# The last tile of the last projection in two token halves, in a two-layer trunk kernel

## The chip, the core and the metric

The kernel runs on one core of one Trainium2 chip. Its engines are TensorE (matmuls, with a separate queue of weight loads), VectorE, ScalarE, GpSimd and SyncE (which issues the DMAs here); the profile calls them PE, PEld, DVE, ACT, POOL and SP. The metric is the device time of one execution in microseconds; lower is better.

## What is computed

Two layers of a trunk over 256 latent tokens with a prefix of 256 context tokens, 1024 channels, in float32. Each layer mixes tokens (a convolution branch and neighbourhood attention, gated) and then channels (a gated MLP with a convolution of width 3 ahead of the activation). The change touches only what ends the last layer: the MLP's down projection, the gated residual and the final RMSNorm of the latent tokens.

```python
def conv_ffn(h, w_up, dw, dw_b, w_down):
    u = dwconv1d(h @ w_up, dw, dw_b)
    a, g = jnp.split(u, 2, axis=-1)
    return (jax.nn.silu(g) * a) @ w_down          # w_down: 2816 x 1024
...
        x = x + g2 * conv_ffn(h2, w_up[l], ffn_dw[l], ffn_dw_b[l], w_down[l])
...
    return rmsnorm(x, final_norm_g)               # x / sqrt(mean(x^2) + 1e-6) * g, over channels
```

## The kernel before

Everything is kept with channels on partitions and tokens along the free axis: the stream `x` is eight tiles `x[n]` of 128 channels by 512 columns, the 256 latent tokens (`LAT`) and then the 256 context tokens (`CTX`). In the last layer the context is no longer needed after its keys and values, so the column range `CTX` of `x` is free there.

Products go through `mm3` (lines 178 to 181): float32 operands are split into a high part, rounded to the type `F32R`, and a low rest, and each product is three matmuls, high by high, high weights by low data, low weights by high data. The weights arrive in units of 128x1024 (eight blocks of 128x128). `wunit` issues the unit's DMA on SP's queue into `raw` (four buffers), ScalarE casts it to `whi` (line 160) and VectorE subtracts to make `wlo` (line 161); both have four buffers.

The down projection of the last layer has eight output tiles `n`, each a sum over `KF` = 22 blocks `k` of the hidden activations `fh[k]`, `fl[k]` (128 hidden channels by 256 tokens, high and low part). In the last layer the whole projection is one pass over `n` in the loop that begins with `for streams, ns in`, with 256 columns a matmul. Block `t = n * KF + k` of the weights is in unit `t // 8`. After every fourth `k` a `slot()` lets side work take a step, here the dot products (line 271) for the gate vector of this sub-layer. After the last `k` of a tile, `residual` (line 898) makes x = x + gate * product on VectorE and hands the result to `SumSq.add`, which accumulates squares: ScalarE squares, VectorE adds to the accumulator `acc`. With `apart` set, the last tile's squares are made by VectorE (line 314) and kept as a part of their own in `parts`, so that the sums over partitions can start with the accumulator. Then line 1078 scales the tile by the final gain on ScalarE, into the free columns `CTX` of `x[n]`. Behind tile 6 one small instruction loads ScalarE's table for the square root.

Behind the loop comes the final norm, for all 256 tokens at once. Line 1094 sums the squares over the partitions: a matmul with the squares of 128 tokens as weights and a column of ones as data, for two parts and two token halves. Line 1098 takes the root on ScalarE, line 1099 the reciprocal on VectorE. Now there is one factor per token, with tokens on partitions; the transposes of line 1102 spread it over all partitions into the bank `po`. Line 1107 multiplies the eight scaled tiles by it, 256 tokens at a time, and SP issues the output: two DMAs of 128 KB (line 1109) and three of 256 KB (line 1111).

Each engine runs its instructions in the order in which they are written, and waits at an instruction until what that needs is there; loads of weights may run ahead of the matmuls before them.

Of the kernel before, what the change touches and what calls it, by code (L numbers as in the profile page):

```python
# [8 lines left out]
F32 = mybir.dt.float32  # L9
F32R = mybir.dt.float32r  # L10
BF16 = mybir.dt.bfloat16
AF = mybir.ActivationFunctionType
ALU = mybir.AluOpType
AX = mybir.AxisListType

P = 128
D = 1024
KD = D // P
DEPTH = 2
S = 256  # L20
# [8 lines left out]
KF = FFN // P  # L29
# [3 lines left out]
LAT, CTX = slice(0, S), slice(S, 2 * S)  # L33

BADA, N1G, DW, DWB, LNG, LNB, N2G, FDW, FDB, NPAR = 0, 48, 56, 180, 184, 188, 192, 200, 332, 376


U_GLU0, U_V, U_IN, U_NA, U_CO, U_WO, U_UP, U_DN = 0, 2, 6, 36, 40, 44, 52, 96
# [7 lines left out]
def trunk(ctx: ExitStack, tc: tile.TileContext, xt, cvec, crow, wall, wada, params, bias_t, rope_t, out):  # L46
    nc = tc.nc
    pe, act, dve, pool, sp = nc.tensor, nc.scalar, nc.vector, nc.gpsimd, nc.sync
# [11 lines left out]
    def nm(s):  # L60
        uid[0] += 1
        return f"{s}_{uid[0]}"
# [3 lines left out]
    def psum(tag="main"):  # L66
        return psp.tile([P, 512], F32, tag=tag, bufs=BANKS[tag], name=nm(tag))

    def tmp(w=512):
        return tp.tile([P, w], F32, tag="t", bufs=5, name=nm("t"))  # L70

    def small(shape, tag, bufs=2):
        return tp.tile(shape, F32, tag=tag, bufs=bufs, name=nm(tag))

    def sl(w, i):
        return w[:, i * P : (i + 1) * P]
# [14 lines left out]
    def whole(g):  # L91

        while True:
            try:
                next(g)
            except StopIteration as e:
                return e.value

    def finish(g):
        for _ in g:  # L100
            pass
        if g in side:
            side.remove(g)


    start = ExitStack()
# [3 lines left out]
    par = cp.tile([P, DEPTH * NPAR + KD], F32, name="par")  # L110
    act.dma_start(par[:, :DW], params[:, :DW])
    ident = cp.tile([P, P], F32, name="ident")
    make_identity(nc, ident)
    one = cp.tile([P, 1], F32, name="one")
# [4 lines left out]
    eps = cp.tile([P, 1], F32, name="eps")  # L119
# [30 lines left out]
    def wparts(l, u, at=None, cuts=2):  # L150

        r = wp.tile([P, UW], F32, tag="raw", bufs=4, name=nm("raw"))
        hi = (at or wp).tile([P, UW], F32R, tag="whi", bufs=4, name=nm("whi"))
        lo = (at or wp).tile([P, UW], F32R, tag="wlo", bufs=4, name=nm("wlo"))
        cs = [slice(i * UW // cuts, (i + 1) * UW // cuts) for i in range(cuts)]
        for c in cs:
            lastdma[0] = sp.dma_start(r[:, c], wall[l, u][:, c])

        def split(c):
            act.copy(hi[:, c], r[:, c])  # L160
            dve.tensor_tensor(lo[:, c], r[:, c], hi[:, c].bitcast(F32), ALU.subtract)  # L161

        def more():
            for c in cs[1:]:
                split(c)

        split(cs[0])
        return (hi, lo), more

    def wunit(l, u, at=None, cuts=1):  # L170
        w, more = wparts(l, u, at, cuts)
        more()
        return w

    def cols(w, i):
        return sl(w[0], i), sl(w[1], i)

    def mm3(ps, w, xh, xl, start, stop):
        pe.matmul(ps, w[0], xh, start=start, stop=False)  # L179
        pe.matmul(ps, w[0], xl, start=False, stop=False)  # L180
        pe.matmul(ps, w[1], xh, start=False, stop=stop)  # L181

    def group(ps, ws, xh, xl, c):

        n = len(ws)
        for k in range(n):
            mm3(ps[:, c], ws[k], xh[k][:, c], xl[k][:, c], k == 0, k == n - 1)
            if k == n // 2 - 1 and c.stop - c.start > S:
                slot()
        slot()  # L190
        return ps

    def unit8(l, u, at=None):
        w = wunit(l, u, at)
        return [cols(w, i) for i in range(KD)]
# [85 lines left out]
    def mod2(l, part, k):  # L281
        return mods[l][:, part * KD + k, :]

    def mod(l, part, k, s):
        return mod2(l, part, k)[:, s : s + 1]
# [12 lines left out]
    x = [xp.tile([P, 2 * S], F32, name=f"x{k}") for k in range(KD)]  # L298
# [26 lines left out]
    def sum_squares(n, T, apart=False):  # L325

        at = tp.tile([P, 512], F32, tag="ss", name=nm("ss"))
        return [SumSq(T, at[:, i * T : (i + 1) * T], apart) for i in range(n)]
# [25 lines left out]
    def h_tiles():  # L354
        return [[hp.tile([P, 2 * S + 2], F32R, tag=f"h{i}{k}", name=nm("h")) for k in range(KD)] for i in range(2)]
# [176 lines left out]
    for k in range(KD):  # L532
        sp.dma_start(x[k], xt[k])
        q = tmp()
# [23 lines left out]
    for l in range(DEPTH):  # L558
        last = l == DEPTH - 1
        NS = 1 if last else 2  # L560
# [3 lines left out]
        with ExitStack() if last else start as e1a:  # L564
# [68 lines left out]
            with ExitStack() as e1b:  # L633
# [15 lines left out]
                if l == 0:  # L649
# [27 lines left out]
                    def more():  # L677
                        act.copy(wg[0][:, cuts[0]], rg[:, cuts[0]])
                        act.copy(pb, ps)
                        act.copy(wv[0][:, cuts[1]], rv[:, cuts[1]])  # L680
                        act.copy(wg[0][:, cuts[1]], rg[:, cuts[1]])
                        for w, r, c in ((wv, rv, cuts[0]), (wg, rg, cuts[0]), (wv, rv, cuts[1])):
                            low_part(w, r, c)
# [3 lines left out]
                    with tc.issue_after(queue[-1].ins):  # L687
                        ps = whole(sums)
                        queue.append(busy(5))
                    pb = tp.tile([P, 512], F32, tag="ss", name="rstd0")  # L690
# [41 lines left out]
                else:  # L732
                    sp.dma_start(rope, rope_t)
                    pg0 = [psum("sc") for _ in range(2)]
                    for uu in range(2):
                        wg = wunit(l, U_GLU0 + uu)
                        for i in range(2):
                            for kk in range(4):
                                k = 4 * uu + kk
# [59 lines left out]
                n = 0  # L799
# [16 lines left out]
            with ExitStack() as e1c:  # L816
# [71 lines left out]
                for n, pc in branch(U_CO, sh_, sl_):  # L888
                    t = tmp()[:, :T]
# [29 lines left out]
                sss = sum_squares(NS, S)  # L919
# [5 lines left out]
                for n in range(NB):  # L925
                    ps = group(psum(), unit8(l, U_WO + n), *z, ALL)
# [8 lines left out]
                for s in range(NS if held else 0):  # L935
                    for n, w in zip(range(NB, KD), held):
                        c = slice(s * S, (s + 1) * S)
                        ps = psum()
# [11 lines left out]
        with ExitStack() as e2:  # L950
            ef = e2.enter_context(tc.tile_pool(name=f"ef{l}", bufs=1))
# [20 lines left out]
            fh, fl = {}, {}  # L972
# [23 lines left out]
            if last:  # L996
# [3 lines left out]
                for k in range(KD):  # L1000
# [4 lines left out]
                    if k == 4:  # L1005
                        pb = whole(sums)
# [45 lines left out]
                    ffn_out(i - 3, pss[2 * i - 6], pss[2 * i - 5])  # L1052
            if not last:
                h1 = h_tiles()
            sss = sum_squares(NS, S, last)
            NB = 0 if last else KD - 2
            if not last:
                pace[0] = 0.55
# [4 lines left out]
            for streams, ns in [((0, 1), range(NB)), *(((s,), range(NB, KD)) for s in range(NS))]:  # L1063
                wu = None
                c = slice(streams[0] * S, (streams[-1] + 1) * S)
                for n in ns:
                    ps = psum()
                    for k in range(KF):
                        t = n * KF + k
                        if t % 8 == 0 or not wu:  # L1070
                            wu = wunit(l, U_DN + t // 8)
                        mm3(ps[:, c], cols(wu, t % 8), fh[k][:, c], fl[k][:, c], k == 0, k == KF - 1)
                        if k % 4 == 3:
                            slot()
                    for s in streams:
                        residual(sss[s], ps, 5, n, s, s * S)
                    if last:
                        scaled = act.mul(x[n][:, CTX], x[n][:, LAT], par[:, DEPTH * NPAR + n : DEPTH * NPAR + n + 1])
                        if n == KD - 2:
                            with tc.issue_after(scaled.ins):  # L1080
                                act.activation(small([P, 1], "wb", 4), one, AF.Sqrt)
                if not last and streams == (0,):
                    finish(ad)
                if not last and len(streams) == 1:
                    nl = norm(1, sss[streams[0]], 1, 0, N1G, h1, streams, streams[0])
                    add_side(nl)


            if last:
                std, rs = small([P, 2], "red"), small([P, 2], "rs")  # L1090
                pt = psum("pt")
                for i, p in enumerate(sss[0].parts):
                    for t in range(2):
                        pe.matmul(
                            pt[:, t : t + 1], sl(p, t), one, start=i == 0 and t == 0, stop=i == len(sss[0].parts) - 1,
                            skip_group_check=True,
                        )
                act.activation(std, pt[:, 0:2], AF.Sqrt, bias=eps, scale=1.0 / D)
                dve.reciprocal(rs, std)
                pb = psum("po")  # L1100
                for t in range(2):
                    pe.transpose(sl(pb, t), rs[:, t : t + 1].to_broadcast([P, P]), ident)
                for k in range(0, KD, 2):
                    y = tmp()
                    for i in range(2):
                        c = slice(i * S, (i + 1) * S)
                        dve.tensor_tensor(y[:, c], x[k + i][:, CTX], pb[:, LAT], ALU.mult)
                        if k == 0:
                            sp.dma_start(out[0][:, c], y[:, c])
                    if k:  # L1110
                        sp.dma_start(out[k // 2], y)


def _tiles(w):
# [110 lines left out]
```

## Time and profile before

| | us |
|---|---|
| median of 3 runs | 1131.16 |
| lowest, highest | 1129.35, 1134.31 |
| the profiled execution's own time | 1129.86 |
| its span, first to last instruction | 1128.1 |
| TensorE busy | 1113.2 |
| VectorE busy | 909.4 |
| ScalarE busy | 563.3 |
| mean granted TensorE clock | 0.997 of full speed |

In the profile's rows, "L181 PE MATMUL main<-fh,wlo 128*128 128x256 f32" is a matmul from line 181 into the tile `main`, with the weights `wlo` of 128 by 128 and data `fh` of 128 partitions by 256 columns. A number in square brackets, or the last column of a group, is how long the engine sat idle before, and who released it. In groups, the numbers behind the first bar are busy time in us and the mean duration of one in ns. In rows in order of time the first number is the start from the beginning of the span, the second the duration, both in us. Matmuls are pipelined: each lasts longer than the distance to the next, and a row's end is modelled. Plain f32 matmuls appear as two instructions each.

### The profile page before, as it was taken

Reading aid. Unit: us, or ns where it says so; the run is one execution under the profiler, and the core shown is the slowest. Engines: PE = TensorE matmul, PEld = TensorE weight load, DVE = VectorE, ACT = ScalarE, POOL = GpSimd, SP = SyncE. Lnnn points to the kernel's source line nnn. Section 1 sums busy time; section 2 is a strip of 40 time slices with the busy share of each in tenths; the row PEclk is TensorE's granted clock in tenths of the full one; section 3 lists DMA queues with packets and bytes.
Section 4 is the critical chain, followed back from the end, with each engine's and each line's share of the span. In section 5 each row is a group of like instructions: output and inputs, shape, how many; then the busy total and the mean of one; then the engine's idle time right before and its main releaser. Section 6 shows DMA issues by size and latency. Waiting matters only on the chain.

```text
span 1128.1 us, 17731 instructions
## 1 busy us (share of the span) xinstructions
PE 1113.2 (99%) x6828; PEld 963.1 (85%) x6828; DVE 909.4 (81%) x1631; ACT 563.3 (50%) x934; POOL 17.2 (2%) x24
## 2 busy tenths in 40 slices
PE   9999999999999999999999999999999999999997
PEld 6778777787789988888888888989898999999997
DVE  5689999685778788888898555789996898988773
ACT  4347657542333543434443223444677567766642
POOL 0000000000000000000000000000000000000000
PEclk9999999999999999999999999999999999999998
DMA  9823231636734344554556655545433575565771
GB/s 361 283 94 104 75 117 38 205 97 217 245 114 144 114 154 149 168 172 146 172 171 218 224 185 189 175 174 175 153 121 115 181 240 172 187 194 180 217 269 57
DMA packets 53941, 190.83 MB, mean 169 GB/s; under 512 B 6240, under 2 KB 6496, under 8 KB 53856
## 3 DMA queue, kind: packets, MB, share of 16 engines
q1 hardware_dynamic: 53568, 189.65, 51.6%
q8 instruction: 54, 0.88, 0.3%
q14 instruction: 31, 0.25, 0.1%
q10 hardware_dynamic: 288, 0.04, 0.0%
HBM read 188.62 MB, written 1.05 MB: 168 GB/s over the span
## 4 chain that ended last, share of the span: by engine, by line
PE 84%; DVE 10%; DMA 3%; ACT 2%; issue 1%; SPq 0%; DVEq 0%; ACTq 0%
PE main L179 25%; PE main L181 24%; PE main L180 24%; DVE cb L591 4%; PE main L644 4%; DVE wlo L161 2%; DMA raw<-in_wall 1%; PE sc L179 1%; PE sc L181 1%; PE sc L180 1%; PE po L202 1%; PE po L512 1%; DMA x<-in_xt 1%; DMA sb<-in_crow 0%; PE sc L440 0%
## 5 line engine op out<-in xcount | busy, mean ns | idle before, releaser
L179 PE MATMUL main<-h,whi 128*128 128x256 f32 (+1 forms) x1328 | 447.5, 338 | 0.0
L181 PE MATMUL main<-h,wlo 128*128 128x256 f32 (+1 forms) x1328 | 444.0, 335 | 0.5 <-DVE wlo L161 0.5
L180 PE MATMUL main<-h,whi 128*128 128x256 f32 (+1 forms) x1328 | 443.0, 334 | 0.0
L160 ACT CAST whi<-raw 128x1024 fp32r<-128x1024 f32 (+1 forms) x244 | 252.4, 1039 | 286.0 <-PE main L180 127.3
L161 DVE TENSOR_TENSOR wlo<-raw,whi 128x1024 fp32r<-128x1024 f32 (+1 forms) x244 | 293.5, 1209 | 113.9 <-ACT whi L160 107.3
L179 PEld LDWEIGHTS main<-h,whi 128*128 128x128 f32 x1328 | 249.8, 188 | 31.8 <-issue 3.9
L181 PEld LDWEIGHTS main<-h,wlo 128*128 128x128 f32 x1328 | 250.0, 189 | 28.7 <-DVE wlo L161 0.7
L180 PEld LDWEIGHTS main<-h,whi 128*128 128x128 f32 x1328 | 250.3, 189 | 27.9 <-issue 0.2
L591 DVE SCALAR_TENSOR_TENSOR cb<-u,par,cb 128x512 f32<-128x512 f32 (+1 forms) x240 | 140.4, 617 | 1.2
L271 DVE CUSTOM_DVE_ANT_0 t<-raw,sb,par 128x1024 bf16<-128x1024 f32 x100 | 126.8, 1279 | 1.0 <-ACT sb L255 0.8
L180 PE MATMUL main<-fl,whi 128*128 128x256 f32 (+1 forms) x386 | 123.1, 319 | 0.0
L179 PE MATMUL main<-fh,whi 128*128 128x256 f32 (+1 forms) x386 | 123.1, 319 | 0.0
L181 PE MATMUL main<-fh,wlo 128*128 128x256 f32 (+1 forms) x386 | 123.1, 319 | 0.0
L180 PEld LDWEIGHTS main<-fl,whi 128*128 128x128 f32 x386 | 72.8, 189 | 5.6
L181 PEld LDWEIGHTS main<-fh,wlo 128*128 128x128 f32 x386 | 72.8, 189 | 5.5
L179 PEld LDWEIGHTS main<-fh,whi 128*128 128x128 f32 x386 | 72.8, 189 | 5.5
L963 ACT ACTIVATE t<-main,par 128x512 f32<-128x512 f32 (+1 forms) x82 | 50.6, 668 | 40.0 <-PE main L181 39.8
L964 DVE SCALAR_TENSOR_TENSOR t<-main,par,t 128x510 f32<-128x510 f32 (+1 forms) x82 | 47.6, 616 | 10.5 <-ACT t L963 10.1
L967 DVE SCALAR_TENSOR_TENSOR t<-main,par,t 128x510 f32<-128x510 f32 (+1 forms) x82 | 46.6, 611 | 0.0
L366 ACT ACTIVATE h<-t,mod 128x256 fp32r<-128x256 f32 x56 | 25.2, 501 | 35.8 <-DVE t L365 35.8
L898 DVE SCALAR_TENSOR_TENSOR x<-main,mod,x 128x256 f32<-128x256 f32 x48 | 22.1, 480 | 23.4 <-PE main L181 23.2
L644 PE MATMUL main<-whi,h 128*128 128x512 f32 x128 | 40.5, 402 | 0.1
(221 smaller groups left out, 1193.1 us busy)
## 6 DMA issues: line engine op xcount, KB each, us to landing
raw<-in_wall SPq DMA_DIRECT2D x239, 512.0 KB, 4.2
raw<-in_wada SPq DMA_DIRECT2D x88, 512.0 KB, 4.4
bias<-in_bias_t SPq DMA_DIRECT2D x8, 640.0 KB, 4.3
row<-in_wada SPq DMA_DIRECT2D x8, 512.0 KB, 5.1
sb<-in_crow SPq DMA_DIRECT2D x5, 512.0 KB, 5.7
x<-in_xt SPq DMA_DIRECT2D x8, 256.0 KB, 4.1
raw<-in_wall SPq DMA_DIRECT2D x8, 256.0 KB, 7.3
out<-t SPq DMA_DIRECT2D x3, 256.0 KB, 2.1
```

Of the source, the lines that this page charges most:

```text
L160: act.copy(hi[:, c], r[:, c])
L161: dve.tensor_tensor(lo[:, c], r[:, c], hi[:, c].bitcast(F32), ALU.subtract)
L179: pe.matmul(ps, w[0], xh, start=start, stop=False)
L180: pe.matmul(ps, w[0], xl, start=False, stop=False)
L181: pe.matmul(ps, w[1], xh, start=False, stop=stop)
L271: dve.tensor_tensor_reduce(tmp().bitcast(BF16), r, v, 1.0, pr(l, BADA + n, 1), ALU.mult, ALU.add, mods[l][:, n, s : s + 1])
L366: high = act.activation(hi[:, c], y[:, c], AF.Identity, bias=b)
L591: dve.scalar_tensor_tensor(cb[j], src, w, cb[j], ALU.mult, ALU.add)
L644: mm = pe.matmul(pv[t], h1[n == 1][k][:, c], w[n == 2][:, b], start=k + n == 0, stop=k == KD - 1 and n == 2)
L963: act.activation(c, pv_, AF.Identity, bias=pr(l, FDB + t, 1), scale=w[1])
L964: dve.scalar_tensor_tensor(c[:, :, 1:], pv_[:, :, : S - 1], w[0], c[:, :, 1:], ALU.mult, ALU.add)
L967: dve.scalar_tensor_tensor(c[:, :, : S - 1], pv_[:, :, 1:], w[2], c[:, :, : S - 1], ALU.mult, ALU.add)
```

## The change

The loop over output tiles stops ahead of the last one (`n = 7`). That tile runs as two halves of 128 tokens: `half(0)` makes its 22 times 3 products for tokens 0 to 127, then update, scaling and squares of that half; `half(1)` does the same for tokens 128 to 255, with the same weight units, and between its products, behind `k = 7` and `k = 13`, come the norm factor and the output of the first half (`factor(0)`, `give(0)`). Behind the second half come `factor(1)` and `give(1)`. There are no slots within this tile.

The scaled tiles go to a new tile `xs`, laid out by token half, channel tile and token. With it one instruction multiplies four channel tiles of one half (512 elements) by the factor, which is read four times through a broadcast. The output has a layout of its own, in four pieces of 256 KB, two for each half, and the host's last rearrangement follows it. The sums of squares of tiles 0 to 6 use the accumulator alone. The scratch space for descriptors of dynamic DMAs is set to 1024.

```diff
-            sss = sum_squares(NS, S, last)
+            sss = sum_squares(NS, S)
+            if last:
+                xs = ef.tile([P, 2, KD, P], F32, name="xs")
...
                 for n in ns:
+                    if last and n == KD - 1:
+                        break
...
                     if last:
-                        scaled = act.mul(x[n][:, CTX], x[n][:, LAT], par[:, DEPTH * NPAR + n : DEPTH * NPAR + n + 1])
+                        g = par[:, DEPTH * NPAR + n : DEPTH * NPAR + n + 1]
+                        scaled = act.mul(xs[:, :, n, :], x[n][:, LAT].rearrange("p (h t) -> p h t", h=2), g)
...
             if last:
-                std, rs = small([P, 2], "red"), small([P, 2], "rs")
-                pt = psum("pt")
-                for i, p in enumerate(sss[0].parts):
-                    for t in range(2):
-                        pe.matmul(
-                            pt[:, t : t + 1], sl(p, t), one, start=i == 0 and t == 0, stop=i == len(sss[0].parts) - 1,
-                            skip_group_check=True,
-                        )
-                act.activation(std, pt[:, 0:2], AF.Sqrt, bias=eps, scale=1.0 / D)
-                dve.reciprocal(rs, std)
-                pb = psum("po")
-                for t in range(2):
-                    pe.transpose(sl(pb, t), rs[:, t : t + 1].to_broadcast([P, P]), ident)
-                for k in range(0, KD, 2):
-                    y = tmp()
...
+                n = KD - 1
+                g = par[:, DEPTH * NPAR + n : DEPTH * NPAR + n + 1]
+                units = {n * KF // 8: wu}
+                squares = []
+
+                def half(h, between=()):
+                    c = sl(x[n], h)
+                    ps = psum()[:, :P]
+                    for k in range(KF):
+                        t = n * KF + k
+                        if t // 8 not in units:
+                            units[t // 8] = wunit(l, U_DN + t // 8)
+                        mm3(ps, cols(units[t // 8], t % 8), sl(fh[k], h), sl(fl[k], h), k == 0, k == KF - 1)
+                        if k in between:
+                            between[k]()
+                    dve.scalar_tensor_tensor(c, ps, mod(l, 5, n, 0), c, ALU.mult, ALU.add)
+                    act.mul(xs[:, h, n, :], c, g)
+                    q = ef.tile([P, P], F32, name=f"sq{h}")
+                    dve.tensor_tensor(q, c, c, ALU.mult)
+                    squares.append(q)
+
+                rsh = []
+
+                def factor(h):
+                    std, rs = small([P, 1], "red"), small([P, 1], "rs")
+                    pt = psum("pt")
+                    for i, p in enumerate((sl(sss[0].acc, h), squares[h])):
+                        pe.matmul(pt[:, 0:1], p, one, start=i == 0, stop=i == 1)
+                    act.activation(std, pt[:, 0:1], AF.Sqrt, bias=eps, scale=1.0 / D)
+                    dve.reciprocal(rs, std)
+                    rsh.append(rs)
+
+                def give(h):
+                    pb = sl(psum("po"), 0)
+                    pe.transpose(pb, rsh[h].to_broadcast([P, P]), ident)
                     for i in range(2):
...
+                        y = tmp().rearrange("p (k t) -> p k t", k=4)
+                        dve.tensor_tensor(y, xs[:, h, 4 * i : 4 * i + 4, :], pb.unsqueeze(1).to_broadcast([P, 4, P]), ALU.mult)
+                        sp.dma_start(out[h, i], y)
+
+                half(0)
+                half(1, {7: lambda: factor(0), 13: lambda: give(0)})
+                factor(1)
+                give(1)
...
-    nc = bacc.Bacc("TRN2", target_bir_lowering=False, num_devices=1)
+    nc = bacc.Bacc("TRN2", target_bir_lowering=False, num_devices=1, dynamic_dma_scratch_size=1024)
...
-    out = nc.dram_tensor("out_0", (KD // 2, P, 2 * S), F32, kind="ExternalOutput").ap()
+    out = nc.dram_tensor("out_0", (2, 2, P, 4, P), F32, kind="ExternalOutput").ap()
```

More of the change, by code (lines that the diff above doesn't have):

```diff
@@ L1099, in trunk @@
-                dve.reciprocal(rs, std)
-                pb = psum("po")
-                for t in range(2):
-                    pe.transpose(sl(pb, t), rs[:, t : t + 1].to_broadcast([P, P]), ident)
-                for k in range(0, KD, 2):
-                    y = tmp()
-                    for i in range(2):
[L1106 to L1111, printed above, removed]
+                n = KD - 1
@@ L1223 @@
     got = r.results[0]["out_0"]
-    return np.ascontiguousarray(got.reshape(KD // 2, P, 2, S).transpose(0, 2, 1, 3).reshape(D, S).T).reshape(1, S, D).astype(f32, copy=False)
+    return np.ascontiguousarray(got.reshape(2, 2, P, 4, P).transpose(1, 3, 2, 0, 4).reshape(D, S).T).reshape(1, S, D).astype(f32, copy=False)
```

## The prediction

> **What bounds the kernel now.** I read the page first (busy time by engine, shares of the chain that ended last), then the chain of waits of the last 11 us, then the order of time on each engine there, and last the groups by shape for durations.
>
> ```profile
> PE 1113.2 (99%) x6828; PEld 963.1 (85%) x6828; DVE 909.4 (81%) x1631; ACT 563.3 (50%) x934; POOL 17.2 (2%) x24
> ...
> PE 84%; DVE 10%; DMA 3%; ACT 2%; issue 1%; SPq 0%; DVEq 0%; ACTq 0%
> ```
>
> TensorE is busy 99% of the span and carries 84% of the chain, so any step added to its stream goes into the time at its full length. The end is another matter:
>
> ```profile
> 1118.99 0.13 PE main L181
> ...
> 1119.15 0.49 DVE x L898
> ...
> 1119.67 0.44 DVE t L314
> ...
> 1120.15 0.62 PE pt L1094 x4
> ...
> 1120.85 0.27 ACT red L1098
> ...
> 1121.14 0.18 DVE rs L1099
> ...
> 1121.36 0.45 PE po L1102 x2
> ...
> 1121.83 0.42 DVE t L1107
> 1122.26 0.33 DVEq L1220
> 1122.59 1.99 DVE t L1107 x6
> ```
>
> After the last product ends at 1119.12 a strictly serial tail follows: update, square, sums over partitions, root, reciprocal, transposes, eight output products of VectorE up to 1124.58, then the transfers. The span ends at 1128.1, so the tail is 9.0 us: 5.46 to the last output product, 3.5 of transfer and closing behind it. That is all the change can attack; what it pays with is TensorE steps. The last tile's own products:
>
> ```profile
> 1111.12 0.28 PE L179 MATMUL main<-fh,whi 128*128 128x256 f32 x1
> 1118.83 0.28 PE L181 MATMUL main<-fh,wlo 128*128 128x256 f32 x1
> ```
>
> 22 k times 3 is 66 products; from the first start to the last are 65 steps in 7.71 us, 0.1186 us a product of 256 columns, or 7.83 for the tile. The durations in these rows (0.28) overlap; the step is what counts.
>
> **The change, part by part.**
>
> *1. 66 products of 256 columns become 132 of 128 (the main cost).* Each needs its own load of 128x128 weights, for half 1 loads them again. No product of float32r in the trace has fewer than 256 columns, so the step at 128 must be bounded. From below, the column rate:
>
> ```profile
> 301.12 0.39 PE L181 MATMUL main<-sh,wlo 128*128 128x512 f32 x1
> ...
> 302.95 0.39 PE L180 MATMUL main<-sl,whi 128*128 128x512 f32 x1
> ```
>
> Eight steps in 1.83 us are 0.229 for 512 columns, so 256 columns more cost 0.110 (0.43 ns each) and 128 columns would step at 0.1186 - 0.055 = 0.064. But the loads do not shrink:
>
> ```profile
> L202 PEld LDWEIGHTS po<-raw,sil 128*32 128x32 f32 x128 | 3.2, 109 | 4.0 <-issue 2.2 <-ACT whi L680 0.4
> L512 PEld LDWEIGHTS po<-pT,V 128*64 128x64 f32 x144 | 9.5, 136 | 5.4 <-issue 1.3
> L181 PEld LDWEIGHTS main<-fh,wlo 128*128 128x128 f32 x386 | 72.8, 189 | 5.5
> L1094 PEld LDWEIGHTS pt<-one,ss 128*128 128x128 f32 x4 | 0.5, 190 | 0.0
> ...
> 1118.83 0.53 PEld L1094 LDWEIGHTS pt<-one,ss 128*128 128x128 f32 x4
> 1120.14 0.52 PEld L1094 LDWEIGHTS pt<-one,t 128*128 128x128 f32 x4 [0.78 <-DVE t L314]
> ```
>
> A load lasts 109 ns for 32 columns, 136 for 64, 189 for 128: 80 ns for 96 columns more, 0.83 ns a column, so 128 columns occupy the loading path for 107 ns. The last two rows show the same thing as a step: with one moving column there is nothing to compute, yet four loads take 0.53 and 0.52, (0.53 - 0.19) / 3 = 0.113 and (0.52 - 0.19) / 3 = 0.110. Those loads are of plain f32, but last as long (190) as those of float32r (189). At 256 columns load and product cover each other; at 128 the product is the shorter, and the load sets the step. I take 0.112, from the row that it is nearest to: a stream of 128-column loads with too little product to cover them. Ends: 0.064 below; above, two passes as plain f32 has them at just this width:
>
> ```profile
> 6.46 1.06 PE L527 MATMUL pt<-one,t 128*128 128x128 f32 x8
> L527 PE MATMUL pt<-one,t 128*128 128x128 f32 x32 | 4.4, 280 | 0.7 <-DVE t L539 0.5 <-DVE t L542 0.2
> ```
>
> Eight instructions here are four products (two passes each): (1.06 - 0.27) / 7 = 0.113 an instruction, 0.225 a product. With 0.112: 132 x 0.112 = 14.78 against 7.83, **+6.95**. With 0.064: 8.45, +0.6. With 0.225: 29.7, +21.9.
>
> The Trainium skill, "TensorE: Matmul & The Clock Gate", section "LDWEIGHTS (loading the stationary operand)", puts a load at its columns divided by 1.2 GHz, whatever the rows, and so speaks against the change; the slope of 0.83 ns a column agrees with it, and by its figure alone (an estimate, 107 ns) the two halves would take 14.1 instead of 14.78.
>
> *2. The first half's norm on TensorE, inside the second half's products.* Four f32 instructions for the sums and one transpose now stand in the stream.
>
> ```profile
> 736.77 0.58 PE L336 MATMUL pt<-one,ss 128*128 128x1 f32 x4 [1.92 <-DVE ss L322]
> 737.41 0.28 PE L180 MATMUL sc<-h,whi 128*128 128x256 f32 x1
> ...
> 937.86 0.28 PE L181 MATMUL main<-h,wlo 128*128 128x258 f32 x1
> 937.98 0.38 PE L351 MATMUL po<-ident,rs 128*128 128x128 f32 x2
> ...
> 938.32 0.28 PE L180 MATMUL sc<-h,whi 128*128 128x258 f32 x1
> ```
>
> From the start of four such sums to the second product behind them is 0.64; less one product (0.119) they cost 0.52. Two transposes stretch two steps from 0.24 to 0.46, so 0.11 each. **+0.63.** Neither should wait: half 0's update and square end 0.7 us after its last product, the sums come 24 products (2.7 us) after it; root and reciprocal end about 0.5 after the sums, the transpose comes 18 products (2.0 us) after them. If that cover were gone, the products queued behind would wait in order. Ends: 0.4 (nothing but bare steps of 0.08) and 0.9 (0.05 for each of several waits).
>
> *3. The first half's output.* After the transpose 24 products (2.7 us) are left; two output products of VectorE take 1.3 (part 4), and their two transfers are issued on SP's queue, which holds nothing else then:
>
> ```profile
> 1092.26 7.30 SPq L157 DMA_DIRECT2D raw<-in_wall  x4
> 1122.28 0.82 SPq L1109 DMA_DIRECT2D out<-t  x2
> 1123.28 1.66 SPq L1111 DMA_DIRECT2D out<-t  x3
> out<-t SPq DMA_DIRECT2D x3, 256.0 KB, 2.1
> ```
>
> The weights' last issue is over at 1099.56. The work is hidden under TensorE's products, cost 0; uncovered it would be those 1.3 us of VectorE again. The transfers land 2.1 us after issue, before half 1's are due.
>
> *4. The tail behind the second half.* Now each step is for one half of the tokens:
>
> ```profile
> L322 DVE TENSOR_TENSOR ss<-ss,t 128x256 f32<-128x256 f32 x44 | 18.1, 421 | 3.8 <-ACT t L318 3.5
> L322 DVE TENSOR_TENSOR ss<-ss,t 128x512 f32<-128x512 f32 x3 | 2.1, 688 | 0.1
> L1107 DVE TENSOR_TENSOR t<-x,po 128x256 f32<-128x256 f32 x8 | 2.7, 416 | 0.5 <-PE po L1102 0.5
> L1078 ACT ACTIVATE x<-x,par 128x256 f32<-128x256 f32 x8 | 4.0, 497 | 5.5 <-DVE x L898 5.5
> ```
>
> 256 elements more cost 0.267, so 128 fewer save 0.133: update 0.49 to 0.36, square 0.44 to 0.31, together -0.27. Two sums in place of four: -0.23 (two steps of 0.113; the accumulator's part stays beneath the update, as now). One transpose for two: -0.11. Output: now 0.42 + 0.33 + 1.99 = 2.74; then two of 512, the first stepping at 0.33 + 0.27 = 0.60 (today's eight step at (2.74 - 0.42) / 7 = 0.33), the second lasting 0.69: 1.29, so -1.45. Root and reciprocal have fixed lengths. Sum **-2.06**. The last transfer is 256 KB, as now, so the 3.5 us behind it stay; with less ahead of it in the queue it may gain up to 0.3 (the 128 KB ones land in 1.8). Ends: -1.8 and -2.4.
>
> *5. What costs nothing.* Scaling into `xs` keeps one ACT instruction a tile, and ACT idles there 5.5 us before the last. Squares are still added on VectorE for tiles 0 to 6. The dropped slots of the last tile carry no work, and its weights are ready whichever half asks first:
>
> ```profile
> 1096.07 1.28 DVE L271 CUSTOM_DVE_ANT_0 t<-row,sb,par 128x1024 bf16<-128x1024 f32 x1
> ...
> 1107.69 1.05 ACT L160 CAST whi<-raw 128x1024 fp32r<-128x1024 f32 x1 [1.20 <-issue]
> 1108.77 1.23 DVE L161 TENSOR_TENSOR wlo<-raw,whi 128x1024 fp32r<-128x1024 f32 x1 [1.03 <-ACT whi L160]
> ```
>
> The last dot product for the modulation starts at 1096.07; the last unit is split by 1110.0, before the tile begins at 1111.12, and half 1 reuses units 19 to 21 in their buffers (three of four). The list of DMA issues has only SP's and ScalarE's, sized and placed as before but for the outputs; no row shows that the smaller scratch for descriptors enters into their times, and I take zero from both sides.
>
> *Sum:* +6.95 + 0.63 - 2.06 = **+5.5 us** on the profiled execution's 1129.86 (span 1128.1 and 1.8 around it): 1135.4. That execution lies 1.3 below the median of the three runs (1131.16); on the median it is 1136.7. I forecast the middle, **1136**.
>
> **The rivals.**
>
> *A, two passes.* If products of float32r under 256 columns go as plain f32 does, part 1 is +21.9 and the sum +20.5: **1150** (1151.6 on the median). For it: every product of float32r here has 256 columns or more, so nothing shows the fast rate below that. Against it: the rate per column is the same at 512 and 256, and loads of both types last alike.
>
> *B, not slower: the loads are hidden after all.* If a load runs ahead of more than one product, the step falls to between the column rate 0.064 and the middle 0.088 of both bounds. With 0.064: +0.6 + 0.63 - 2.06 = -0.8, **1129.0** (1130.3 on the median); with 0.088: 11.6 - 7.83 = +3.8, sum +2.4, 1132.2. It decides from where 132 steps cost less than 7.83 + 1.43, a step of 0.070. Against it: no row with a 128-column load steps below 0.110. The Trainium skill, same page, section "Back-to-back issue gap", states about 81 ns for sustained pairs of load and product at 128 columns; by that figure, an estimate, the sum would be +1.4, and no row of this trace bears it out for four-byte weights.
>
> *C, the overlap fails.* TensorE waits for half 0's reciprocal in mid stream, or its output comes late and stands in front of half 1's on VectorE and SP. The margins are 1.5 us at the transpose and 1.4 for the output; if both were used up, the sum is +5.5 + 1.3 or more, 1137 to 1138.
>
> **How the numbers follow.** A measurement of this kernel tells about 0.5% from no change, 5.66 us. The load-bound case gets 0.62; its own range, steps of 0.107 to 0.1186 (14.1 to 15.7) with the ends of parts 2 and 4, is +4.3 to +6.9, so 1134 to 1138 with the medians' offset: it straddles that bound, 0.30 above, 0.32 within. A gets 0.22 (slower), C 0.02 (slower), B 0.11, all within. For faster by 5.66 us the tail of 9.0 would have to shrink to about 3 at no cost; no row gives that, 0.03. So slower 0.54, same 0.43, faster 0.03. The range runs from B's lower end on the median to A: 1130 to 1152.
>
> **What would show it.** In the changed profile: 128-column products of `fh`, `fl` stepping at 0.11 (0.06 for B, 0.22 for A) with loads of 189 ns back to back; the last tile taking about 15.4 us with the norm inside it; sums and transpose of half 0 without a wait in front of them; two output transfers issued before the last product; 3.4 us from the last product to the last output product, 3.5 behind it. I am wrong if the step is under 0.10 or over 0.125, or if the tail keeps more than 8 us.

## The result, and the profile after

| | before | after |
|---|---|---|
| median, us | 1130.74 (10 runs) | 1135.58 (10 runs) |
| lowest, highest | 1128.73, 1134.31 | 1133.88, 1140.24 |
| profiled span | 1128.1 | 1134.0 |

The ratio is 1.0045, with a 95% interval from 1.0031 to 1.0059: the change costs 5.1 us of 1130.74 (3.5 to 6.7; the medians alone lie 4.84 apart). That is clear of zero, and within the half per cent (5.66 us) that the prediction named as its bound, though the interval reaches over it.

The first question to the changed profile is at what distance the products of 128 columns follow each other. In order of time on TensorE (start, duration), at the beginning of the last tile, where the second half begins, and at the first half's sums and transpose:

```profile
1112.06 0.22 PE L179 MATMUL main<-fh,whi 128*128 128x128 f32 x1
1112.12 0.27 PE L180 MATMUL main<-fl,whi 128*128 128x128 f32 x1
...
1119.38 0.27 PE L179 MATMUL main<-fh,whi 128*128 128x128 f32 x1
...
1122.06 0.33 PE L1122 MATMUL pt<-one,ss 128*128 128x1 f32 x2
1122.25 0.36 PE L1122 MATMUL pt<-one,sq 128*128 128x1 f32 x2
...
1124.52 0.29 PE L1129 MATMUL po<-ident,rs 128*128 128x128 f32 x1
```

The first half's 66 products begin at 1112.06, the second half's at 1119.38: 7.32 us, 0.111 us a product where 256 columns had 0.1186. Half the work takes 94% of the time. The sums and the transpose of the first half stand in the stream without a gap in front of them (1122.06, 1124.52, no idle time in brackets). The groups by shape show that the loads are what they were:

```profile
L181 PEld LDWEIGHTS main<-fh,wlo 128*128 128x128 f32 x408 | 77.0, 189 | 5.6
```

A load still lasts 189 ns. Now the tail, in the chain of waits:

```profile
1127.48 0.36 DVE x L1110
...
1127.86 0.30 DVE sq L1113
...
1128.21 0.40 PE pt L1122 x2
...
1128.69 0.27 ACT red L1123
1128.98 0.17 DVE rs L1124
...
1129.29 0.31 PE po L1129
```

Update, square, sums and transpose are shorter than their counterparts before, root and reciprocal are as long, and the two output products end at 1130.91 (on VectorE, in order of time, with the first half's pair and the transfers):

```profile
1124.84 1.29 DVE L1132 TENSOR_TENSOR t<-xs,po 128x512 f32<-128x512 f32 x2 [1.68 <-PE po L1129]
...
1129.63 1.28 DVE L1132 TENSOR_TENSOR t<-xs,po 128x512 f32<-128x512 f32 x2 [0.48 <-PE po L1129]
...
1125.56 5.71 SPq L1133 DMA_DIRECT2D out<-t  x4
```

A clean way to compare two executions here is from the update of tile 6, after which nothing differs but the change, to the end of the span (which is printed to 0.1 us, so such a difference is good to about 0.1). Before, that update starts at 1111.32 and the span ends at 1128.1: 16.78. After:

```profile
1112.26 0.48 DVE L898 SCALAR_TENSOR_TENSOR x<-main,mod,x 128x256 f32<-128x256 f32 x1 [1.32 <-PE main L181]
...
1127.48 0.35 DVE L1110 SCALAR_TENSOR_TENSOR x<-main,mod,x 128x128 f32<-128x128 f32 x1 [1.35 <-PE main L181]
```

1134.0 - 1112.26 = 21.74, so +4.96, which agrees with the ratio. The spans differ by 0.94 more, because tile 6's update is that much later; that has nothing to do with the change. Tables by stretch (length, busy time of TensorE, its loads, VectorE, ScalarE, GpSimd, granted clock, DMA share, GB/s) show where it arose, first before, then after:

```profile
936.00:938.00 2.00, 2.00 (x19) 2.00 (x19) 1.31 (x3) 0.61 (x1) 0.70 (x1) 1.00 0.77 244
```

```profile
936.00:938.00 2.00, 2.00 (x11) 2.00 (x11) 1.22 (x1) 0.30 (x1) 0.33 (x1) 0.50 0.73 250
```

In the 4 us ahead of these rows both wait for the norm between two projections (TensorE busy 2.48 and 2.05 of 4 us); in the profiled execution of after the clock fell to 0.50 behind that wait, in that of before it did not. ScalarE's casts of the weights, matched one by one, start 0.88 earlier in after at 925 and 0.95 later from 957 on, and then keep that distance up to the last tile. The experiments below start their tile 6 update anywhere from 1109.0 to 1114.9, so this is what executions differ by.

### The profile page after: what moved, and what is told of

It reads as the page before. It is cut to its first block, busy times and chain, and to the rows that moved or that the text cites. A ratio compares the mean times of both kernels' runs of the same rounds, so it can differ in the third digit from the quotient of the medians.

```text
span 1134.0 us, 17863 instructions
## 1 busy us (share of the span) xinstructions
PE 1121.8 (99%) x6894; PEld 971.2 (86%) x6894; DVE 909.7 (80%) x1630; ACT 564.1 (50%) x936; POOL 15.7 (1%) x24
## 4 chain that ended last, share of the span: by engine, by line
PE 85%; DVE 9%; DMA 2%; ACT 2%; issue 1%; SPq 0%; DVEq 0%; ACTq 0%
PE main L179 25%; PE main L181 25%; PE main L180 25%; DVE cb L591 4%; PE main L644 4%; DVE wlo L161 2%; PE sc L179 1%; PE sc L181 1%; PE sc L180 1%; DMA raw<-in_wall 1%; PE po L202 1%; PE po L512 1%; DMA x<-in_xt 1%; PE sc L440 0%; DMA sb<-in_crow 0%
## 5 line engine op out<-in xcount | busy, mean ns | idle before, releaser
L179 PE MATMUL main<-fh,whi 128*128 128x256 f32 (+2 forms) x408 | 128.9, 316 | 0.0
L180 PE MATMUL main<-fl,whi 128*128 128x256 f32 (+2 forms) x408 | 128.8, 316 | 0.0
L181 PE MATMUL main<-fh,wlo 128*128 128x256 f32 (+2 forms) x408 | 128.8, 316 | 0.0
L179 PEld LDWEIGHTS main<-fh,whi 128*128 128x128 f32 x408 | 77.0, 189 | 5.6
L181 PEld LDWEIGHTS main<-fh,wlo 128*128 128x128 f32 x408 | 77.0, 189 | 5.6
L180 PEld LDWEIGHTS main<-fl,whi 128*128 128x128 f32 x408 | 77.0, 189 | 5.5
L989 ACT CAST fh<-t 128x256 fp32r<-128x256 f32 (+1 forms) x43 | 21.9, 510 | 36.4 <-DVE t L979 35.9
```

## The experiments

All build on the changed kernel unless they say otherwise. Beside the ratio each is read by the time from tile 6's update to the end of the span (before 16.78, after 21.74), from its own profile; the runs with 64, 96 and 192 columns and with two-byte weights are one execution each and have no ratio.

### The scratch alone

The kernel before with one edit:

```diff
-    nc = bacc.Bacc("TRN2", target_bir_lowering=False, num_devices=1)
+    nc = bacc.Bacc("TRN2", target_bir_lowering=False, num_devices=1, dynamic_dma_scratch_size=1024)
```

> The kernel before with the smaller scratch for descriptors and nothing else. Theory: no effect, ratio to before 1.000 within its interval, and the last tile starts where it did within the 1 to 2 us that executions differ by. Rival (the scratch or the moved tiles caused the 0.9 us by which the changed kernel's last tile started later): ratio 1.001, last tile again about 0.9 later.

Ratio 0.9999 (0.9986 to 1.0012). Tile 6's update starts at 1113.47 and the span ends at 1130.2: 16.73. The start is 2.15 later than in the profile of before, but the ratio shows no cost of that kind, and the changed kernels of the other experiments, all with the small scratch, start it from 2.3 earlier to 3.6 later: it is the spread of executions. The scratch does nothing to the tail; a cost under 1.4 us ahead of it is not excluded by the interval, but nothing points to one.

### Whole products, the rest in halves

```diff
-                half(0)
-                half(1, {7: lambda: factor(0), 13: lambda: give(0)})
-                factor(1)
-                give(1)
+                whole_tile()          # 66 products of 256 columns, then update, scale, square of each half
+                factor(0)
+                factor(1)
+                give(0)
+                give(1)
```

> The last tile's products run whole again, 66 of 256 columns; update, squares, norm and output stay in halves, all behind the products. Theory (the loads of the 66 additional products cost the time, the tail in halves saves some): the products of the tile take 7.8 us in place of 15.1, the tail from the first update to the last output product about 4.8 (changed kernel 3.4, before 5.4), so 5 to 6 us faster than the changed kernel and 0.3 to 1.0 faster than before: ratio to before 0.999 to 1.000. Rival (the time went into something else that came with the change, the new layout, the wide output products or the scratch): it stays near the changed kernel, ratio to before 1.003 to 1.005.

Ratio 1.0001 (0.9991 to 1.0010). VectorE and TensorE in order of time:

```profile
1111.01 0.48 DVE L898 SCALAR_TENSOR_TENSOR x<-main,mod,x 128x256 f32<-128x256 f32 x1 [1.32 <-PE main L181]
...
1118.84 0.61 DVE L1109 SCALAR_TENSOR_TENSOR x<-main,mod,x 128x128 f32<-128x128 f32 x2 [6.44 <-PE main L181]
...
1121.57 1.26 DVE L1131 TENSOR_TENSOR t<-xs,po 128x512 f32<-128x512 f32 x2
1123.47 1.29 DVE L1131 TENSOR_TENSOR t<-xs,po 128x512 f32<-128x512 f32 x2 [0.63 <-PE po L1128]
```

```profile
1122.98 0.45 PE L1128 MATMUL po<-ident,rs 128*128 128x128 f32 x1 [1.72 <-DVE t L1131]
```

From update to update 7.83 us, exactly as before: with the products whole again the 4.9 us are gone (16.89 to the end), while the layout, the wide output products and the scratch stayed. So the time went into the products. The tail missed its expectation: 5.92 to the last output product where 4.8 was expected. The second transpose waited 1.72 us for VectorE, since `po` is one bank and the first half's output products still read it; and both reciprocals stood ahead of the first output product on VectorE.

### Two banks

```diff
-                    pb = sl(psum("po"), 0)
+                    pb = sl(psum("po" if h == 0 else "sc"), 0)
...
+                factor(0)
+                spread(0)             # the transpose, apart from the output products
+                give(0, 0)
+                factor(1)
+                spread(1)
+                give(0, 1)
...
```

> As with whole products and the norm and output in halves behind them, but the second half's factor goes to a PSUM bank of its own, and the first half's first output product stands ahead of the second half's reciprocal on VectorE. Theory (with one bank the second transpose waited for the first half's output products): from the first update to the last output product about 4.7 us (one bank 5.9, before 5.4); from the update of tile 6 to the end of the span 15.7 to 16.3 (before 16.8, changed kernel 21.7), so 0.5 to 1.1 us faster than before, ratio 0.999 to 1.000, which the interval may not tell from 1. Rival (the transfers end the kernel, whatever VectorE does): 16.8 again.

The edit does two things: a bank for each half, and another order of the output products. Ratio 0.9985 (0.9975 to 0.9996).

```profile
1113.93 0.48 DVE L898 SCALAR_TENSOR_TENSOR x<-main,mod,x 128x256 f32<-128x256 f32 x1 [1.33 <-PE main L181]
...
1121.76 0.61 DVE L1109 SCALAR_TENSOR_TENSOR x<-main,mod,x 128x128 f32<-128x128 f32 x2 [6.43 <-PE main L181]
...
1124.41 0.16 DVE L1123 RECIPROCAL rs<-red 128x1 f32<-128x1 f32 x1 [0.85 <-ACT red L1122]
1124.49 1.26 DVE L1135 TENSOR_TENSOR t<-xs,po 128x512 f32<-128x512 f32 x2
1125.67 1.28 DVE L1135 TENSOR_TENSOR t<-xs,sc 128x512 f32<-128x512 f32 x2
```

The gap between the two pairs of output products is gone; to the last of them it is 5.19 (before 5.43), to the end of the span 16.37, 0.41 better than before, and just short of the 15.7 to 16.3 expected. The reciprocal of the second half still runs ahead of the first output product, whatever the order in the source, and TensorE takes the second half's sums (1123.41) ahead of the first half's transpose (1123.88). So the engines do not always run in the order in which the kernel is written, as the description of the kernel before has it, and the intended order was not tested; 4.7 was not reached. 0.41 of 1131.6 is 0.9996, the upper end of the interval; what else the measured 0.9985 holds the profile does not show. This is the one version with all its products whose interval lies below 1, by little.

### The overlap taken away

```diff
-                half(1, {7: lambda: factor(0), 13: lambda: give(0)})
-                factor(1)
-                give(1)
+                half(1)
+                factor(0)
+                factor(1)
+                give(0)
+                give(1)
```

> Products in halves as in the changed kernel, but the norm and the output of the first half stand behind all products. Theory: the stream gets 0.54 us shorter (four sums and a transpose less), the tail to the last output product longer by about 1.1 (two more output products of VectorE, 0.6 each, minus what root and sums hide), the transfers by 0.1 to 0.2: 0.6 to 0.8 us slower than the changed kernel, so the overlap is worth less than 1 us. Rival (the overlap is worth the whole norm and output of a half): 2.5 us slower or more.

Ratio 1.0048 (1.0035 to 1.0060), beside 1.0045 of the changed kernel.

```profile
1110.76 0.48 DVE L898 SCALAR_TENSOR_TENSOR x<-main,mod,x 128x256 f32<-128x256 f32 x1 [1.32 <-PE main L181]
...
1125.44 0.35 DVE L1110 SCALAR_TENSOR_TENSOR x<-main,mod,x 128x128 f32<-128x128 f32 x1 [6.69 <-PE main L181]
...
1128.77 1.29 DVE L1132 TENSOR_TENSOR t<-xs,po 128x512 f32<-128x512 f32 x2 [0.63 <-PE po L1129]
```

From tile 6's update to the second half's 14.68 (changed kernel 15.22): the norm in the stream cost 0.54. From there to the last output product 4.62 (3.43). To the end of the span 1133.2 - 1110.76 = 22.44, +0.70, as the theory had it. The ratios alone, 0.0003 apart with intervals of more than 0.001 to each side, would not show it. By the profile the first half's norm and output beneath the second half's products are worth 0.7 us.

### 64, 96 and 192 columns

The step of 0.111 at 128 columns has two readings: the load sets it, or products under 256 columns run at two passes a column (128 x 2 x 0.43 ns is 0.110). One step of the changed kernel already speaks against the second: its first narrow product, behind one of 256 columns, is followed after 0.06 (1112.06 to 1112.12), near 128 x 0.43 ns, while the loads around it keep their distance (1111.95, 1112.07, 1112.17, 1112.29). Other widths tell more.

```diff
-                    ps = psum()[:, :P]
-                    for k in range(KF):
...
+                    for j in range(2):
+                        d = slice(64 * j, 64 * j + 64)                  # 96 columns: 32 * j, 32 * j + 96
+                        e = slice(P * h + 64 * j, P * h + 64 * j + 64)
+                        for k in range(KF):
...
+                            mm3(ps[:, d], cols(units[t // 8], t % 8), fh[k][:, e], fl[k][:, e], k == 0, k == KF - 1)
```

> The last tile in four quarters: 264 products of 64 columns in place of 132 of 128, each with its load of 128x128. Theory (the load sets the step, whatever the columns): step 0.111 again, the tile's products 29.3 us, the time 14.7 above the changed kernel. Rival (products under 256 columns run at two passes a column: 128 x 2 x 0.43 ns is 0.110 as well, so the changed kernel's step doesn't tell them apart): step 0.055, 14.5 us, no change of time.

> Each half's products take 192 columns, 64 of them computed for nothing. Theory (load): step 0.111, at most 0.115, the tile's products as in the changed kernel, time within 0.6 us of it. Rival (two passes a column under 256): 192 x 2 x 0.43 ns is 0.165, the tile's products 21.8 us, 7 us slower.

> The last tile in four passes of 96 columns (a third of them computed twice): 264 products. Theory (load sets the step, and the clock halved with 64 columns because the array itself was busy only 0.24 of a step): step 0.111 with the array busy 0.36 of it; if that still counts as busy the clock stays at 1.00 and the tile's products take 29.3 us, 15 us above the changed kernel; if not, the clock halves after some 3 us and they take about 55, as with 64 columns. Rival for the 64-column run (its slow clock was a chance of that run): clock 1.00 here.

With 192 columns (64 of each half computed for nothing) the one execution took 1136.97. Three products on TensorE near the tile's beginning (the middle one left out) and tile 6's update:

```profile
1113.11 0.27 PE L180 MATMUL main<-fl,whi 128*128 128x192 f32 x1
...
1113.33 0.28 PE L179 MATMUL main<-fh,whi 128*128 128x192 f32 x1
...
1113.22 0.48 DVE L898 SCALAR_TENSOR_TENSOR x<-main,mod,x 128x256 f32<-128x256 f32 x1 [1.32 <-PE main L181]
```

Two steps in 0.22, so 0.111 again, and 1135.2 - 1113.22 = 21.98 to the end, 0.24 from the changed kernel: 50% more columns for nothing more. With 64 columns, TensorE in order of time:

```profile
1109.05 0.28 PE L179 MATMUL main<-fh,whi 128*128 128x64 f32 x1
1109.16 0.28 PE L180 MATMUL main<-fl,whi 128*128 128x64 f32 x1
...
1112.20 0.40 PE L179 MATMUL main<-fh,whi 128*128 128x64 f32 x1
1112.41 0.40 PE L180 MATMUL main<-fl,whi 128*128 128x64 f32 x1
```

At first the step is 0.111 again, so two passes a column (0.055 here, 0.165 at 192) are out, and the step does not depend on the columns, which fits the load. But the time was 1172.04, 36 above the changed kernel's and not 15: from 1112 on the step is 0.213. The table by stretch says why, for 64 and for 96 columns:

```profile
1110.00:1112.00 2.00, 2.00 (x20) 2.00 (x19) 0.39 (x1) 1.81 (x3) 0.00 (x0) 0.98 0.00 0
1112.00:1115.00 3.00, 3.00 (x17) 3.00 (x16) 0.00 (x0) 0.00 (x0) 0.00 (x0) 0.50 0.00 0
```

```profile
1112.00:1114.00 2.00, 2.00 (x20) 2.00 (x20) 0.43 (x1) 1.99 (x3) 0.00 (x0) 1.00 0.00 0
...
1116.00:1118.00 2.00, 2.00 (x12) 2.00 (x11) 0.00 (x0) 0.00 (x0) 0.00 (x0) 0.50 0.00 0
```

TensorE shows as busy all the time, yet its granted clock halves after 3.1 and 3.7 us of narrow products (from 1108.79 to 1111.92 at 64 columns, from 1111.28 to 1115.01 at 96), and the loads slow down with it. Both widths did it (96 columns took 1174.01), so it was no chance of the one run; at 128, in the changed kernel, the clock stays:

```profile
1118.00:1120.00 2.00, 2.00 (x20) 2.00 (x20) 0.38 (x2) 0.03 (x1) 0.00 (x0) 1.00 0.04 8
```

### Two-byte weights

```diff
-                        mm3(ps, cols(units[t // 8], t % 8), sl(fh[k], h), sl(fl[k], h), k == 0, k == KF - 1)
+                        up = [v.bitcast(BF16)[:, 1::2] for v in (*cols(units[t // 8], t % 8), sl(fh[k], h), sl(fl[k], h))]
+                        mm3(ps, up[:2], up[2], up[3], k == 0, k == KF - 1)
```

> Only the upper two bytes of weights and data are read in the last tile, as bfloat16 with a step of two elements; the rest of the mantissas is left out. Theory (it is the load of four-byte weights that takes 0.111): loads get shorter than 189 ns and the step falls under 0.10, towards the column rate 0.055; the tile's products take 7.5 to 12 us in place of 14.7. Rival (a pair of load and product has a floor of 0.111 for 128 columns of weights, whatever the type): step 0.111, no change.

One execution, 1129.46. TensorE, a load and tile 6's update:

```profile
1113.05 0.22 PE L179 MATMUL main<-fh,whi 128*128 128x128 bf16 x1
1113.11 0.22 PE L180 MATMUL main<-fl,whi 128*128 128x128 bf16 x1
...
1113.05 0.10 PEld L180 LDWEIGHTS <-whi 128*128 128x128 bf16 x1
1113.05 0.48 DVE L898 SCALAR_TENSOR_TENSOR x<-main,mod,x 128x256 f32<-128x256 f32 x1 [1.32 <-PE main L181]
```

Loads last 0.10 and the step is 0.057, so there is no floor of 0.111 for a pair of load and product as such: it belongs to four-byte operands (weights and data both changed here; the next experiment shows that it is the load). To the end of the span it is 1127.7 - 1113.05 = 14.65, 2.13 under before: with loads that the products cover, the halves would have paid. That is rival B's world (its lower bound was 0.064), and a stream of float32r pairs is not in it. The Trainium skill, "TensorE: Matmul & The Clock Gate", gives 81 ns for such pairs at 128 columns in its section "Back-to-back issue gap"; neither type does that here, 111 for four bytes and 57 for two.

### Two loads a block in place of three

```diff
+                        pe.matmul(ps.rearrange("p (a t) -> p a t", a=2), hi, fboth[k][:, :, cc], start=k == 0, stop=False)
+                        pe.matmul(ps[:, :P], lo, fboth[k][:, 0, cc], start=False, stop=k == KF - 1)
...
+                    dve.scalar_tensor_tensor(c, ps[:, P:], mod(l, 5, n, 0), c, ALU.mult, ALU.add)
+                    dve.scalar_tensor_tensor(c, ps[:, :P], mod(l, 5, n, 0), c, ALU.mult, ALU.add)
```

> In the last tile the high and the low data of a half stand side by side and go as one product of 256 columns with the high weights, so that a block costs two loads and not three; VectorE adds the two sums in two updates. Theory (count of loads): 44 pairs of 0.1186 + 0.111 are 10.1 us in place of 14.7, and one update more in the tail is +0.35: 4 to 4.5 us faster than the changed kernel, ratio to before 1.000 to 1.001. Rival (the cost is in the number of columns or of accumulations, not of loads): no gain.

Ratio 1.0005 (0.9992 to 1.0019).

```profile
1114.87 0.33 PE L1113 MATMUL main<-fhl,whi 128*128 128x256 f32 x1
1115.04 0.22 PE L1114 MATMUL main<-fhl,wlo 128*128 128x128 f32 x1
1115.10 0.33 PE L1113 MATMUL main<-fhl,whi 128*128 128x256 f32 x1
...
1114.92 0.19 PEld L1114 LDWEIGHTS main<-fhl,wlo 128*128 128x128 f32 x1
1115.04 0.19 PEld L1113 LDWEIGHTS main<-fhl,whi 128*128 128x128 f32 x1
1115.15 0.19 PEld L1114 LDWEIGHTS main<-fhl,wlo 128*128 128x128 f32 x1
...
1114.89 0.48 DVE L898 SCALAR_TENSOR_TENSOR x<-main,mod,x 128x256 f32<-128x256 f32 x1 [1.32 <-PE main L181]
```

A block of both costs 0.23 and not 3 x 0.111, and to the end of the span it is 1132.4 - 1114.89 = 17.51: 4.23 less than the changed kernel, inside the 4 to 4.5 expected. With as many columns as before, taking a third of the loads (and of the products) away takes most of the loss away, 4.23 of 4.96. The rows also say what keeps the time: the loads stand 0.11 to 0.12 apart, while the products between them are followed after 0.17 (256 columns) and 0.06 (128 columns) in turn. A four-byte product of 128 columns that is followed after 0.06 has neither two passes a column nor a floor of 0.111 of its own; the distance of the loads is what stays.

## Why the prediction was right

The forecast was 1136 and +5.5; the measured median is 1135.58, and the ratio gives +5.1. The forecast leaned to a change beyond its bound of 5.66 us (0.54) over one within it (0.43); the measured one is within. Term by term, from the profiles:

| term | predicted | measured | from |
|---|---|---|---|
| products in halves | +6.95 | +6.85 | 14.68 without the norm (overlap taken away) - 7.83 |
| first half's norm in the stream | +0.63 | +0.54 | 15.22 - 14.68 |
| tail to the last output product | -2.06 | -2.00 | 3.43 - 5.43 |
| transfers and closing | 0 | -0.43 | 3.09 - 3.52 |
| sum | +5.5 | +4.96 | 21.74 - 16.78 |

*Part 1* was right for its reason: the step at 128 columns is 0.111, predicted 0.112 from f32 loads with one moving column. That this is the load's doing, and not two passes a column or a floor for each product, is shown by the other widths and by the run with two loads a block, where products of 128 columns step at 0.06 between loads 0.11 to 0.12 apart. Rival A itself (0.225) is out by the first profile, B (0.064 to 0.088) too, for this type of data.

*Part 2* was 0.09 too large; no wait stood in front of sums or transpose, so C did not happen. *Part 3* held: the first half's two output products (1124.84 to 1126.13) and the issue of both transfers lie under the second half's products. Taking that cover away cost 1.19 in the tail (4.62 - 3.43) and gave 0.54 back in the stream, 0.7 net to the end of the span.

*Part 4* held to 0.06. The mis-sized term is the one behind it, "the last transfer is 256 KB, as now, so the 3.5 us behind it stay": they shrank to 3.09. The prediction allowed a gain of 0.3 there, from transfers with less ahead of them. That is not where it came from: the last transfer is issued within 0.03 of the last output product's end in both and lands 2.1 later in both. What shrank lies behind the landing, in SP's last instructions (the page of after, then line 1220 of before and line 1247 of after):

```profile
out<-t SPq DMA_DIRECT2D x4, 256.0 KB, 2.1
...
L1220 SPq DRAIN  x3: 7/7/130, 1126.9 to 1127.6; - x3
...
L1247 SPq DRAIN  x3: 7/7/7, 1133.3 to 1133.6; - x3
```

From the landing to the end it is 1.4 before and with the scratch alone, 1.0 in every run with the new output, which is nearly all of the 0.43. So it is neither the scratch nor the overlap; whether the number of transfers (five, now four) or their layout does it, no run separates. In the run with two banks the four transfers follow each other closely, the last lands after 2.3, and the 3.5 become 3.35.

*Part 5*, nothing from the scratch, held as far as its own run can tell.

## What to carry to other kernels

Before splitting a product with four-byte weights into narrower ones, look at what the load of its weights costs beside it: below the width where product and load cover each other, narrower products save next to nothing (here 0.111 at 64, 128 and 192 columns beside 0.1186 at 256), and the split pays the price again. Then weigh that against what the overlap can really save, here 0.7 us of VectorE and root behind the last product. A serial tail can be cut into halves without touching the products, if each half has its own PSUM bank; here that gained 0.41 us by the profile.

## What the runs showed of the hardware that was not expected

A stream of products without a single gap lost half its clock. The array's own share of a step is the columns times 0.43 ns over 0.111: about 0.25 at 64 columns, 0.37 at 96, just under 0.50 at 128. The first two, one execution each, fell to a granted clock of 0.50 after 3.1 and 3.7 us and stayed there for the 50 us left of the tile, the third never did in this tile. The loads follow that clock (step 0.111 to 0.213), so a narrow split can cost twice what its loads suggest. The Trainium skill, same page, section "Part 1: The HAM clock gate (the "warmup" mystery)", ties the half clock to idle windows of about 3.4 us; the time until the drop agrees, but here TensorE's queue was never idle, which suggests, and does not prove, that what is watched is nearer to the array's work than to the queue. Where between 0.37 and 0.50 it decides was not tried, so how close the changed kernel stands to that edge is open.
